# Input and memory projections in plain fp32, block transposes over 128 partitions, and one more complex product on GpSimd, in an S5 and gated-delta encoder layer

## The chip, the cores and the metric

The kernel runs on one core of a Trainium2 chip. The metric is the device time of one execution in microseconds (us). Names of engines: PE is TensorE's matmul stream and PEld its weight loads, DVE is VectorE, ACT is ScalarE, POOL is GpSimd, SP is SyncE, whose queue (SPq) issues most transfers.

## What is computed

One encoder layer on 512 tokens of width 1024, all in fp32. The part that the change touches, cut to what matters:

```python
h = rmsnorm(x, norm_mix)
u, q, k, v, z, beta_f, beta_b, a_f, a_b = split_cols(h @ w_in)   # 512, 4 x 512, 16 gate columns
y_s5  = s5_mixer(u, ...)     # two complex scans over time (forward, backward), gelu, GLU
y_gdn = gdn_mixer(q, k, v, z, beta_f, ...)   # conv of 5 taps, silu, l2norm; per chunk of 64 tokens:
#   l_mat = strict_lower(k_beta @ k.T) * decay
#   u_c, w_c = triangular_solve(l_mat, v_beta), triangular_solve(l_mat, k_beta * exp(g))
#   then a recurrence over the chunks, in both directions
x = x + concat([y_s5, y_gdn]) @ w_out
x = x + mem_xattn(rmsnorm(x, norm_xattn), rmsnorm(mem, norm_mem), wq, wk, wv, wo)   # mem: 256 x 1024
x = x + hier_moe(rmsnorm(x, norm_moe), ...)   # 32 experts, top 2 in the top group
return rmsnorm(x, norm_final)
```

## The kernel before

The order of each engine's instructions is set by the tile framework's scheduler, which starts from the program's order; several generators are interleaved into that by `weave` (L42). So the order is decided anew whenever the program changes.

**Stage A** (`stage_a`, `rms_T` L107): the tokens are loaded, normed and transposed on PE, 8 blocks of 128 features. Each block leaves PSUM twice: ACT writes it rounded to fp32r (`hth`, L129), DVE writes the rest (`htl`, L130).

**Projections.** A projection (`proj`, L180) makes 128 columns of h @ w_in for all 512 tokens. `wsplit` (L135) loads 128 columns of weights (512 KB) through SP's queue into `wst` (two buffers), ACT casts them to fp32r (`whi`, L142), and DVE or POOL subtracts (`wlo`, L143). Which of the two is set by `lo_eng`: POOL for the first two and in the memory units, DVE for the convolutions' projections. `mm3` (L146) then does three fp32r matmuls for each of 8 blocks of features: L150 (whi with htl), L151 (whi with hth), L152 (wlo with hth), 24 in all. There are 20 projections: 4 of u, 12 of q, k and v, and 4 of z. The gates (L540) are 16 matmuls with fp32 operands over `htl` and `hth`, four at a time in row groups of PE's columns.

**S5 parameters** (`s5_params`): among much else a loop of 8 turns, each with two complex products (`cmul`, L221, six operations of 128x512, L225 to L230), `pm` and `ca`. The tables `CA_ENG` and `PM_ENG` (L54) say which engine does one: 0 is DVE, 1 is POOL. Woven with it are the convolutions of q, k and v (`gdn_conv`: PE's projection, two evictions on ACT, four DVE operations at L641, silu on ACT).

**Triangular inverse** (`gdn_inv`, L686): the matrix N is built from the keys; the 32x32 diagonal blocks are transposed on DVE (`NT`, L731, four transposes, one for each 32 partitions), inverted by a recursion of 31 steps on DVE (a product, L739, and a subtraction, L741), and the result is transposed again (`XT` L748, `XN` L749, four each). PE then makes the off-diagonal blocks (L767 on) and the chain can begin. Woven with it are the S5 recursion (`s5_rec`, four small DVE operations a step, L414 to L417), the z projections, and the memory units.

**Memory units** (`mem_kv`, L945): 16 units, each 128 columns of the memory's keys or values: one `wsplit` with the subtraction on POOL, 24 fp32r matmuls of 256 columns with `mth` and `mtl`, an eviction, for values two transposes, and a store (L962, on SP's queue). The units that aren't done by then are woven with the chain.

**Chain** (`gdn_chain`, L839 on): the recurrence over chunks, small matmuls with evictions between. After it and the last memory unit a stack of pools closes (`r1`, with the weights and the memory's tiles); S5's output (`s5_out`, L446) loads `tz` (L430) into the space. Then follow the GLU (L475, fp32 matmuls), the mixing product, the cross-attention (whose own split, `wsplit4`, is another function) and the MoE, whose weights are streamed in.

Of the kernel before, what the change touches and what calls it, by code (L numbers as in the profile page):

```python
# [9 lines left out]
F32 = mybir.dt.float32  # L10
F32R = mybir.dt.float32r
BF16 = mybir.dt.bfloat16
I32 = mybir.dt.int32
U32 = mybir.dt.uint32
AF = mybir.ActivationFunctionType
OP = mybir.AluOpType
# [15 lines left out]
P = 128  # L32
T = 512
D = 1024
# [16 lines left out]
            live.remove(s)  # L51


CA_ENG = (0, 1, 0, 1, 0, 1, 0, 1)  # L54
PM_ENG = (1, 0, 1, 0, 1, 0, 1, 0)


class Enc:
    def __init__(self, ctx, tc, A, out):
        self.ctx, self.tc, self.nc, self.A, self.out = ctx, tc, tc.nc, A, out  # L60
        self.lo_eng = self.nc.vector
        self.banks, self.turn = {}, {}
        self.loads = []

# [39 lines left out]
        return t  # L104


    def rms_T(self, pool, tiles, gain, hi, lo, tag, between=None, junk=None):  # L107

        nc = self.nc
        n = len(tiles)  # L110
        ss = pool.tile([P, 8], F32, name=tag + "ss", bufs=1)
        rs = pool.tile([P, 8], F32, name=tag + "rs", bufs=1)
        xn = []
        for i, t in enumerate(tiles):
            sq = junk if junk is not None else pool.tile([P, D], BF16, name=tag + "sq", bufs=1)
            nc.scalar.activation(sq, t, AF.Square, accum_out=ss[:, i:i + 1])
            nc.vector.tensor_scalar(ss[:, i:i + 1], ss[:, i:i + 1], 1.0 / D, 1e-6, op0=OP.mult, op1=OP.add)
            nc.gpsimd.tensor_tensor(rs[:, i:i + 1], ss[:, i:i + 1], self.nhalf[:, 0:1], op=OP.pow)
            nc.vector.tensor_scalar(t, t, rs[:, i:i + 1], None, op0=OP.mult)
            xn.append(t)  # L120
        if between:
            between()
        for k in range(8):
            ps = self.ps("tp")
            for i in range(n):
                nc.tensor.transpose(ps[:, i * P:(i + 1) * P],
                                    xn[i].rearrange("t (p k) -> t k p", k=8)[:, k, :], self.ident)
            src = ps[:, :n * P]
            nc.scalar.activation(hi[:, k, :], src, AF.Copy, scale=gain[:, k:k + 1])  # L129
            nc.vector.scalar_tensor_tensor(lo[:, k, :], src, gain[:, k:k + 1], hi[:, k, :].bitcast(F32),  # L130
                                           op0=OP.mult, op1=OP.subtract)
        return xn


    def wsplit(self, src, w, lo_eng=None, tag="w"):  # L135

        nc, wp = self.nc, self.wp
        st = wp.tile([P, 8, w], F32, name="wst", tag=tag + "st", bufs=2)
        nc.sync.dma_start(st, src)
        hi = wp.tile([P, 8, w], F32R, name="whi", tag=tag + "hi", bufs=2)  # L140
        lo = wp.tile([P, 8, w], F32R, name="wlo", tag=tag + "lo", bufs=2)
        nc.scalar.activation(hi, st, AF.Copy)  # L142
        (lo_eng or self.lo_eng).tensor_tensor(lo, st, hi.bitcast(F32), op=OP.subtract)  # L143
        return hi, lo

    def mm3(self, ps, pairs, first=True, last=True):  # L146

# [7 lines left out]
    def stage_a(self):  # L155
        nc, tc, A = self.nc, self.tc, self.A
        pool = self.pa
        gain = self.col8('norm_mix', self.cp)
        x2d = A['x'][0]
        xt = []  # L160
        with tc.tile_pool(name="xp", bufs=1) as xp:
            for i in range(4):
                t = xp.tile([P, D], F32, name=f"x{i}")
                nc.sync.dma_start(t, x2d[i * P:(i + 1) * P, :])
                xt.append(t)
            self.hth = pool.tile([P, 8, T], F32R, name="hth")
            self.htl = pool.tile([P, 8, T], F32R, name="htl")
            self.pre = {}

            def first_weights():  # L170
                for c0 in (0, P):
                    self.pre[c0] = self.wsplit(self.w_in(c0, P), P, nc.gpsimd)
                self.w_g = self.wp.tile([P, 8, 16], F32, name="wg", bufs=1)
                nc.sync.dma_start(self.w_g, self.w_in(2560, 16))

            self.rms_T(xp, xt, gain, self.hth, self.htl, "h", first_weights)

    def w_in(self, c0, w):
        return self.A['w_in'][0].rearrange("(p k) n -> p k n", k=8)[:, :, c0:c0 + w]

    def proj(self, c0):

        hi, lo = self.pre.get(c0) or self.wsplit(self.w_in(c0, P), P)
        ps = self.ps("mm")
        self.mm3(ps, [((hi[:, k, :], lo[:, k, :]), (self.hth[:, k, :], self.htl[:, k, :])) for k in range(8)])
        return ps

    def proj_u(self):
# [328 lines left out]
    def gates(self):  # L517
        nc, A, tc = self.nc, self.A, self.tc
        v = nc.vector
# [4 lines left out]
        with tc.tile_pool(name="gt_", bufs=1) as tp:  # L524
# [6 lines left out]
            ps = self.ps("s5")  # L531
# [2 lines left out]
            sel = tp.tile([P, 16], F32, name="gsel")  # L534
            v.tensor_reduce(sel, self.ident.rearrange("p (i c) -> p c i", i=4)[:, :16], axis=AX.X, op=OP.add)
            for j in range(2):
                for part in (self.htl, self.hth):
                    for i in range(4):
                        k = j * 4 + i
                        nc.tensor.matmul(ps[i * 32:i * 32 + 16], self.w_g[:, k], part[:, k].bitcast(F32),  # L540
                                         start=(j == 0 and part is self.htl), stop=(j == 1 and part is self.hth))
            for i in range(4):
                nc.scalar.activation(gT[i * 32:i * 32 + 16], ps[i * 32:i * 32 + 16], AF.Copy)
            pt = self.ps("tp")
# [4 lines left out]
            y, ab, e, w, t1 = (tp.tile([P, 4, 8], F32, name="s" + n) for n in "yaewt")  # L549
# [42 lines left out]
            for hf in range(2):  # L592
                s = slice(hf * 64, hf * 64 + 64)
                f, b = slice(hf, 8, 2), slice(7 - hf, None, -2)
# [92 lines left out]
    def gdn_inv(self):  # L687
        nc, tc = self.nc, self.tc
# [4 lines left out]
        if True:  # L693
# [31 lines left out]
            Ni = N.rearrange("p d b h f -> p (d b h) f")  # L725
            NT = tp.tile([P, 32, 32], F32, name="NT", tag="NT")
            X = tp.tile([P, 32, 32], F32, name="X", tag="X")
            for q in range(4):
                s = slice(q * 32, q * 32 + 32)
                b = q % 2  # L730
                v.transpose(NT[s], Ni[s, :, b * 32:b * 32 + 32].rearrange("p i f -> p f i"))  # L731
            ii = tp.tile([P, 32, 32], I32, name="ii", tag="pd")
            g_.iota(ii, pattern=[[1, 32], [-1, 32]], base=0, channel_multiplier=0)
            v.tensor_scalar(X, ii, 0.0, None, op0=OP.is_equal)
# [8 lines left out]
                    yield  # L743
            XT = tp.tile([P, 32, 32], F32, name="XT", tag="NT")
            XN = tp.tile([P, 32, 32], F32, name="XN", tag="pd")
            for q in range(4):
                s = slice(q * 32, q * 32 + 32)
                v.transpose(XT[s].rearrange("p n i -> p i n"), X[s])  # L748
                v.transpose(XN[s].rearrange("p n j -> p j n"), X[s].rearrange("p i j -> p j i"))  # L749

            R = tp.tile([P, 32, 32], F32, name="R", tag="X")
            lh = self.lhc.rearrange("p n h (e c) -> p n h e c", e=2)
# [180 lines left out]
    def mem_norm(self):  # L933
        nc, A = self.nc, self.A
        gain = self.col8('norm_mem', self.cp)
        self.mth = self.mp.tile([P, 8, 256], F32R, name="mth")
        self.mtl = self.mp.tile([P, 8, 256], F32R, name="mtl")

        place = self.U.rearrange("p k r g -> p (k r g)")
        mt = [place[:, i * D:(i + 1) * D] for i in range(2)]  # L940
        for i, t in enumerate(mt):
            nc.sync.dma_start(t, A['mem'][0, i * P:(i + 1) * P, :])
        self.rms_T(self.mp, mt, gain, self.mth, self.mtl, "m", junk=place[:, 2 * D:2 * D + D // 2].bitcast(BF16))

    def mem_kv(self):  # L945
        nc, A, tc = self.nc, self.A, self.tc
        wk = A['xa_wk'][0].rearrange("(p k) n -> p k n", k=8)
        wv = A['xa_wv'][0].rearrange("(p k) n -> p k n", k=8)
        for which, w in ((0, wk), (1, wv)):
            for n in range(8):  # L950
                hi, lo = self.wsplit(w[:, :, n * P:(n + 1) * P], P, nc.gpsimd)
                ps = self.ps("mm")
                self.mm3(ps[:, :256], [((hi[:, k], lo[:, k]), (self.mth[:, k], self.mtl[:, k])) for k in range(8)])
                o = self.wp.tile([P, 256], F32, name="kvo", bufs=2)
                nc.scalar.activation(o, ps[:, :256], AF.Copy)
                if which:
                    pt = self.ps("tp")
                    for m in range(2):
                        nc.tensor.transpose(pt[:, m * P:(m + 1) * P], o[:, m * P:(m + 1) * P], self.ident)
                    o = self.wp.tile([P, 256], F32, name="kvt", bufs=2)  # L960
                    nc.scalar.activation(o, pt[:, :256], AF.Copy)
                nc.sync.dma_start(self.kv_scr[which, :, n], o)  # L962
                yield
# [548 lines left out]
    def build(self):  # L1512
# [41 lines left out]
        with tc.tile_pool(name="gi", bufs=2) as gi:  # L1554
            qkv = self.gdn_in([(w, n, h) for h in range(4) for w, n in ((1, "k"), (0, "q"))] +
                              [(2, "v", h) for h in range(4)], gi)
            s5 = self.s5_params()
            self.lo_eng = nc.gpsimd
            next(s5)
            for _ in u:  # L1560
                pass
            self.lo_eng = nc.vector
            weave((qkv, 13), (s5, 9))

        self.lo_eng = nc.gpsimd
        self.gp2 = pool(left, "gp2")
        self.gp3 = pool(left, "gp3")
        self.gv = pool(gv, "gv", **rt)
# [196 lines left out]
```

## Time and profile before

| what | us |
|---|---|
| median of 3 runs | 927.62 (926.51 to 932.28) |
| the profiled execution | 929.45 |
| its span in the trace | 927.3 |
| mean granted TensorE clock | 0.903 of full speed |

A row of the page or of the trace gives times from the start of the span. Busy time is time in which an engine worked on an instruction; PE's is modelled, since matmuls are pipelined. PEclk is the granted clock as a share of full speed. In brackets behind an instruction stands how long its engine was idle before it and what ended that.

### The profile page before, as it was taken

The page shows a single profiled execution, that of the slowest core. Times are in us where ns is not written, and L with a number is a line of the kernel's source. Part 1 is how long each engine was busy: PE and PEld are TensorE (multiplying, and loading weights), DVE is VectorE, ACT ScalarE, POOL GpSimd, SP SyncE. Part 2 cuts the span into 40 slices and gives each one's busy share as a digit, 9 for nine tenths or more (in the row PEclk, how much of TensorE's full clock was granted, in tenths as well). Part 3 has the DMA queues.
Part 4 walks back from the last instruction along what each step waited for, and adds up shares of the span by engine and source line. Part 5 has one row for each costly group of instructions (what it writes and reads, how often), then busy time and mean ns, then how long its engine had stood idle before and what let it go on. Part 6 is the DMA issues. An engine that isn't in the chain of part 4 may idle for free. (4 is left out here: it accounts for less than half of the span.)

```text
span 927.3 us, 13626 instructions
## 1 busy us (share of the span) xinstructions
PE 781.3 (84%) x5023; PEld 547.1 (59%) x5024; DVE 471.9 (51%) x1060; ACT 367.2 (40%) x801; POOL 302.0 (33%) x254
## 2 busy tenths in 40 slices
PE   5898898898772998899899999996699798778791
PEld 4586576677672975677488888996333343233230
DVE  5599989879999975224653444414300110010026
ACT  6555356565432534633551654432232321121123
POOL 3234687634461411200452223232311111010026
PEclk9998798999896787959899999998799999898896
DMA  8855222222451207611763623597799999999952
GB/s 205 140 86 123 94 92 71 84 60 70 120 168 53 76 18 137 137 46 47 234 215 114 245 96 121 183 405 290 269 394 409 414 412 406 404 406 403 410 223 116
DMA packets 129029, 185.39 MB, mean 200 GB/s; under 512 B 38818, under 2 KB 93090, under 8 KB 125120
## 3 DMA queue, kind: packets, MB, share of 16 engines
q1 hardware_dynamic: 124640, 176.50, 56.7%
q0 software_dynamic: 4320, 8.00, 2.4%
q8 instruction: 40, 0.66, 0.3%
q14 instruction: 29, 0.24, 0.1%
HBM read 165.50 MB, written 26.71 MB: 207 GB/s over the span
## 5 line engine op out<-in xcount | busy, mean ns | idle before, releaser
L1344 PE MATMUL bank<-mw,xt 128*64 128x512 f32 x400 | 114.1, 609 | 1.7 <-ACT yd L1390 1.3
L1348 DVE SCALAR_TENSOR_TENSOR hs<-hs,tw,bank 128x256 f32<-128x256 f32 x16 | 7.7, 480 | 173.1 <-ACT hs L1347 173.1
L143 POOL TENSOR_TENSOR wlo<-wst,whi 128x1024 fp32r<-128x1024 f32 x24 | 58.0, 2420 | 57.6 <-ACT whi L142 44.7
L150 PE MATMUL bank<-htl,whi 128*128 128x512 f32 x160 | 69.3, 434 | 6.2 <-ACT cv L639 3.1
L1344 PEld LDWEIGHTS bank<-mw,xt 128*64 128x64 f32 x400 | 38.5, 143 | 55.9 <-issue 49.9
L152 PE MATMUL bank<-hth,wlo 128*128 128x512 f32 x160 | 67.4, 422 | 0.3 <-DVE wlo L143 0.3
L151 PE MATMUL bank<-hth,whi 128*128 128x512 f32 x160 | 67.2, 420 | 0.0
L973 POOL TENSOR_TENSOR wlo<-wst,whi 128x1024 fp32r<-128x1024 f32 x16 | 38.4, 2404 | 80.8 <-ACT whi L972 80.8
L1347 ACT ACTIVATE hs<-bank,tw 128x256 f32<-128x256 f32 x16 | 7.6, 473 | 137.1 <-PE bank L1344 137.1
L1385 PE MATMUL bank<-mw,hT 128*64 128x512 f32 x120 | 45.7, 664 | 10.9 <-DMA mw<-in_moe_w_down_dram 9.3
L1324 POOL DMA_INDIRECT xg<-t_scr,tidx x16 | 16.4, 1024 | 115.7 <-PE bank L1331 101.4
L142 ACT ACTIVATE whi<-wst 128x1024 fp32r<-128x1024 f32 x36 | 38.2, 1060 | 28.2 <-DMA wst<-in_w_in_dram 9.9
L641 DVE SCALAR_TENSOR_TENSOR cv<-xp,taps,cv 128x512 f32<-128x512 f32 x48 | 46.5, 971 | 0.4
L152 PE MATMUL bank<-mth,wlo 128*128 128x256 f32 x128 | 40.1, 313 | 7.7 <-POOL wlo L143 7.7
L1391 POOL DMA_INDIRECT y_scr<-yd,didx x14 | 14.0, 1001 | 93.5 <-ACT yd L1390 25.0
L150 PE MATMUL bank<-mtl,whi 128*128 128x256 f32 x128 | 40.0, 312 | 3.4 <-ACT zt L683 3.4
L150 PEld LDWEIGHTS bank<-htl,whi 128*128 128x128 f32 x160 | 33.1, 207 | 14.4 <-ACT cv L639 3.8
L1334 ACT ACTIVATE xt<-bank,gm 128x128 f32<-128x128 f32 x128 | 35.0, 391 | 15.4 <-PE bank L1331 15.1
L151 PE MATMUL bank<-mth,whi 128*128 128x256 f32 x128 | 38.9, 304 | 0.0
L152 PEld LDWEIGHTS bank<-hth,wlo 128*128 128x128 f32 x160 | 32.6, 204 | 8.2 <-DVE wlo L143 0.7
L151 PEld LDWEIGHTS bank<-hth,whi 128*128 128x128 f32 x160 | 33.0, 206 | 6.7 <-issue 0.2
L150 PE MATMUL bank<-wlo,oh 128*128 128x256 f32 x128 | 36.6, 289 | 0.0
(570 smaller groups left out, 2219.9 us busy)
## 6 DMA issues: line engine op xcount, KB each, us to landing
mw<-in_moe_w_gate_dram SPq DMA_DIRECT2D x50, 512.0 KB, 13.0
mw<-in_moe_w_up_dram SPq DMA_DIRECT2D x50, 512.0 KB, 12.6
mw<-in_moe_w_down_dram SPq DMA_DIRECT2D x15, 1024.0 KB, 13.8
wst<-in_w_in_dram SPq DMA_DIRECT2D x20, 512.0 KB, 4.3
xl<-in_moe_w_down_dram SPq DMA_DIRECT2D x5, 1024.0 KB, 12.1
ol<-in_moe_w_down_dram SPq DMA_DIRECT2D x5, 1024.0 KB, 13.7
xh<-in_moe_w_down_dram SPq DMA_DIRECT2D x5, 1024.0 KB, 13.3
ca_scr<-ca SPq DMA_DIRECT2D x8, 512.0 KB, 2.7
```

The source lines that it names most:

```text
L142: nc.scalar.activation(hi, st, AF.Copy)
L143: (lo_eng or self.lo_eng).tensor_tensor(lo, st, hi.bitcast(F32), op=OP.subtract)
L150: self.nc.tensor.matmul(ps, ah, bl, start=(first and i == 0), stop=False)
L151: self.nc.tensor.matmul(ps, ah, bh, start=False, stop=False)
L152: self.nc.tensor.matmul(ps, al, bh, start=False, stop=(last and i == n - 1))
L641: v.scalar_tensor_tensor(cv, xp[:, w:w + T], taps[:, w, m:m + 1], cv, op0=OP.mult, op1=OP.add)
L973: nc.gpsimd.tensor_tensor(lo, st, hi.bitcast(F32), op=OP.subtract)
L1324: self.gather = g_.indirect_dma_start(out=xg, out_offset=None, in_=self.t_scr, in_offset=bass.IndirectOffsetOnAxis(ap=self.tidx[:, q:q + 1 ...
L1334: nc.scalar.activation(xt[:, k], ps[:, (k % 4) * P:(k % 4 + 1) * P], AF.Copy, scale=self.gm[:, k:k + 1])
L1344: nc.tensor.matmul(pg[w * 64:w * 64 + 64].rearrange("p (a n) -> p a n", a=2), xt[:, k, w * 64:w * 64 + 64], un[k // 4 * 2 + w][:, :, k % 4 ...
L1385: nc.tensor.matmul(py[w * 64:w * 64 + 64], hT[:, k, w * 64:w * 64 + 64], wd[w][:, k, c], start=(k == 0), stop=(k == 1))
L1391: nc.gpsimd.indirect_dma_start(out=self.y_scr, out_offset=bass.IndirectOffsetOnAxis(ap=self.didx[:, q:q + 1], axis=0), in_=y, in_offset=No ...
```

## The change

`rms_T` writes one fp32 tile (`ht`, `mt`) in place of a pair; its evictions alternate between ACT and DVE. `wcols` only loads the weights, into four buffers in place of two. `mm8` does 8 fp32 matmuls in place of the 24 of `mm3`; the gates take 8 matmuls in place of 16. The casts and subtractions of weights in projections and memory units go, and with them `lo_eng`. `NT` takes three transposes (one of 128 partitions, two of 32), `XT` and `XN` one of 128 partitions each. In the S5 loop POOL does nine of the 16 complex products in place of eight. The split products of the cross-attention and the mixing stay.

```diff
-CA_ENG = (0, 1, 0, 1, 0, 1, 0, 1)
-PM_ENG = (1, 0, 1, 0, 1, 0, 1, 0)
+CA_ENG = (1, 1, 0, 1, 1, 1, 0, 1)
+PM_ENG = (0, 0, 1, 0, 1, 0, 1, 0)
...
-            nc.scalar.activation(hi[:, k, :], src, AF.Copy, scale=gain[:, k:k + 1])
-            nc.vector.scalar_tensor_tensor(lo[:, k, :], src, gain[:, k:k + 1], hi[:, k, :].bitcast(F32),
-                                           op0=OP.mult, op1=OP.subtract)
+            if k % 2:
+                nc.vector.tensor_scalar(out[:, k, :], src, gain[:, k:k + 1], None, op0=OP.mult)
+            else:
+                nc.scalar.activation(out[:, k, :], src, AF.Copy, scale=gain[:, k:k + 1])
...
-    def wsplit(self, src, w, lo_eng=None, tag="w"):
-
-        nc, wp = self.nc, self.wp
-        st = wp.tile([P, 8, w], F32, name="wst", tag=tag + "st", bufs=2)
-        nc.sync.dma_start(st, src)
-        hi = wp.tile([P, 8, w], F32R, name="whi", tag=tag + "hi", bufs=2)
-        lo = wp.tile([P, 8, w], F32R, name="wlo", tag=tag + "lo", bufs=2)
-        nc.scalar.activation(hi, st, AF.Copy)
-        (lo_eng or self.lo_eng).tensor_tensor(lo, st, hi.bitcast(F32), op=OP.subtract)
-        return hi, lo
+    def wcols(self, src, w):
+
+        t = self.wp.tile([P, 8, w], F32, name="wst", bufs=4)
+        self.nc.sync.dma_start(t, src)
+        return t
+
+    def mm8(self, ps, w, act):
+
+        for k in range(8):
+            self.nc.tensor.matmul(ps, w[:, k, :], act[:, k, :], start=(k == 0), stop=(k == 7))
...
-        self.mm3(ps, [((hi[:, k, :], lo[:, k, :]), (self.hth[:, k, :], self.htl[:, k, :])) for k in range(8)])
+        self.mm8(ps, w, self.ht)
...
-                for part in (self.htl, self.hth):
-                    for i in range(4):
-                        k = j * 4 + i
-                        nc.tensor.matmul(ps[i * 32:i * 32 + 16], self.w_g[:, k], part[:, k].bitcast(F32),
-                                         start=(j == 0 and part is self.htl), stop=(j == 1 and part is self.hth))
+                for i in range(4):
+                    k = j * 4 + i
+                    nc.tensor.matmul(ps[i * 32:i * 32 + 16], self.w_g[:, k], self.ht[:, k], start=(j == 0), stop=(j == 1))
...
-            for q in range(4):
+            nd = lambda b: Ni[:, :, b * 32:b * 32 + 32].rearrange("p i f -> p f i")
+            v.transpose(NT, nd(0))
+            for q in (1, 3):
                 s = slice(q * 32, q * 32 + 32)
-                b = q % 2
-                v.transpose(NT[s], Ni[s, :, b * 32:b * 32 + 32].rearrange("p i f -> p f i"))
+                v.transpose(NT[s], nd(1)[s])
...
-            for q in range(4):
-                s = slice(q * 32, q * 32 + 32)
-                v.transpose(XT[s].rearrange("p n i -> p i n"), X[s])
-                v.transpose(XN[s].rearrange("p n j -> p j n"), X[s].rearrange("p i j -> p j i"))
+            v.transpose(XT.rearrange("p n i -> p i n"), X)
+            v.transpose(XN.rearrange("p n j -> p j n"), X.rearrange("p i j -> p j i"))
...
-                hi, lo = self.wsplit(w[:, :, n * P:(n + 1) * P], P, nc.gpsimd)
                 ps = self.ps("mm")
-                self.mm3(ps[:, :256], [((hi[:, k], lo[:, k]), (self.mth[:, k], self.mtl[:, k])) for k in range(8)])
+                self.mm8(ps[:, :256], self.wcols(w[:, :, n * P:(n + 1) * P], P), self.mt)
```

## Rows read from the trace of the kernel before

**Rows 1.** The page's first part: busy us of each engine, its share of the span, and its number of instructions.

```profile
PE 781.3 (84%) x5023; PEld 547.1 (59%) x5024; DVE 471.9 (51%) x1060; ACT 367.2 (40%) x801; POOL 302.0 (33%) x254
```

**Rows 2.** The table of windows: from and to, length, then busy us and number of instructions of PE, PEld, DVE, ACT and POOL, then PEclk, the DMA engines' mean busy share, and GB/s.

```profile
16.00:40.70 24.70, 21.40 (x116) 15.03 (x114) 12.49 (x36) 11.04 (x18) 6.53 (x5) 1.00 0.87 137
40.70:72.00 31.30, 30.94 (x137) 25.29 (x137) 30.05 (x98) 17.55 (x32) 11.56 (x12) 0.95 0.65 100
...
16.00:238.00 222.00, 194.24 (x1508) 150.02 (x1506) 190.57 (x379) 122.44 (x257) 115.00 (x97) 0.92 0.40 92
246.00:293.00 47.00, 28.98 (x224) 27.14 (x222) 47.00 (x147) 13.04 (x19) 21.81 (x9) 0.90 0.42 122
293.00:317.00 24.00, 18.08 (x308) 17.36 (x308) 23.30 (x32) 12.60 (x22) 6.22 (x4) 0.71 0.29 86
317.00:464.00 147.00, 133.27 (x879) 99.80 (x880) 75.17 (x213) 63.75 (x134) 33.40 (x48) 0.81 0.40 101
600.00:927.00 327.00, 261.01 (x1332) 128.50 (x1330) 60.10 (x144) 81.49 (x237) 68.43 (x59) 0.91 0.90 354
```

**Rows 3.** DVE's timeline in 246 to 293 us: start, duration, engine, line, operation, output and inputs, shapes. The first and the last row are the recursion's first product and last subtraction.

```profile
246.17 0.18 DVE L739 TENSOR_TENSOR pd<-NT,X 128x31 f32<-128x31 f32 x1
...
251.14 2.42 DVE L414 TENSOR_TENSOR rt<-a8r,U 128x64 f32<-128x64 f32 x1
...
254.56 0.21 DVE L414 TENSOR_TENSOR rt<-a8r,U 128x64 f32<-128x64 f32 x1
...
292.45 0.18 DVE L741 TENSOR_TENSOR X<-X,pd 128x31 f32<-128x31 f32 x1
```

**Rows 4.** POOL's timeline in the same stretch.

```profile
251.04 2.45 POOL L143 TENSOR_TENSOR wlo<-wst,whi 128x1024 fp32r<-128x1024 f32 x1 [0.44 <-ACT whi L142]
```

**Rows 5.** The weights' subtraction (L143). The first row is POOL's group in the table by line for 246 to 293 us, the second DVE's group in that for 40.7 to 196: shapes, number, busy us and mean ns, idle time before. The third is POOL's row in the tile's own view: number, shortest, median and longest ns, first and last start.

```profile
L143 POOL TENSOR_TENSOR wlo<-wst,whi 128x1024 fp32r<-128x1024 f32 x9 | 21.8, 2423 | 16.8 <-ACT whi L142 16.8
...
L143 DVE TENSOR_TENSOR wlo<-wst,whi 128x1024 fp32r<-128x1024 f32 x12 | 17.6, 1468 | 4.2 <-ACT whi L142 4.2
...
L143 POOL TENSOR_TENSOR wlo<-wst,whi x24: 2334/2378/2853, 11.9 to 324.8; 128x1024 fp32r<-128x1024 f32 x24
```

**Rows 6.** Transposes and other block operations on DVE and POOL. The first row is from DVE's timeline (four transposes one after the other in 7.89 us), the others from the views of single tiles and lines, with number, shortest, median and longest ns, first and last start, and from the timeline again.

```profile
237.98 7.89 DVE L731 STREAM_TRANSPOSE NT<-N 32x1024 f32<-32x1024 f32 x4
...
L748 DVE STREAM_TRANSPOSE XT<-X x4: 1885/1915/2059, 292.7 to 304.1; 32x1024 f32<-32x1024 f32 x4
L749 DVE STREAM_TRANSPOSE XN<-X x4: 1921/2020/2046, 294.5 to 306.0; 32x1024 f32<-32x1024 f32 x4
...
L656 DVE TENSOR_TENSOR vc<-bank,beta x8: 672/688/695, 192.7 to 225.1; 64x512 f32<-64x512 f32 x8
...
170.12 0.68 DVE L227 TENSOR_TENSOR pm<-aF,b 128x512 f32<-128x512 f32 x1
...
L230 POOL TENSOR_TENSOR ca<-ca,P x4: 1712/1724/1737, 91.8 to 179.3; 128x512 f32<-128x512 f32 x4
L230 DVE TENSOR_TENSOR ca<-ca,P x4: 679/1134/1768, 77.2 to 164.4; 128x512 f32<-128x512 f32 x4
```

**Rows 7.** PE's timeline after the recursion: start, duration of the group, and in brackets the idle time before it and what ended that.

```profile
298.37 3.62 PE L767 MATMUL bank<-XT,N 32*32 32x32 f32 x64 [17.25 <-DVE XT L748]
...
306.32 2.21 PE L767 MATMUL bank<-XT,N 32*32 32x32 f32 x64
...
317.43 0.77 PE L839 MATMUL bank<-vc,lhc 128*128 128x128 f32 x2 [0.97 <-ACT whi L142]
```

**Rows 8.** PE's timeline in three places: 23 matmuls of a split projection that follow on each other (the first and the last of them), 17 of a memory unit (the first and the last), and fp32 matmuls of the GLU, 8 records; then the GLU's row in the line's own view (number of records, shortest, median and longest ns).

```profile
196.58 0.39 PE L151 MATMUL bank<-hth,whi 128*128 128x512 f32 x1
...
201.59 0.39 PE L152 MATMUL bank<-hth,wlo 128*128 128x512 f32 x1
...
247.11 0.28 PE L152 MATMUL bank<-mth,wlo 128*128 128x256 f32 x1
...
249.02 0.28 PE L150 MATMUL bank<-mtl,whi 128*128 128x256 f32 x1
...
448.96 3.70 PE L475 MATMUL bank<-gt,wglu 128*128 128x512 f32 x8
...
L475 PE MATMUL bank<-gt,wglu x32: 592/592/1062, 438.3 to 463.0; 128*128 128x512 f32 x32
```

**Rows 9.** PE's timeline: the first and the last of the gates' four groups.

```profile
27.77 1.05 PE L540 MATMUL bank<-htl,wg 128*16 128x512 f32 x8
...
30.36 1.04 PE L540 MATMUL bank<-hth,wg 128*16 128x512 f32 x8
```

**Rows 10.** The view of the tile `htl` on PE in 16 to 72 us: the projections' matmuls with their number, shortest, median and longest ns, first and last start.

```profile
L150 PE MATMUL bank<-htl,whi x56: 387/389/776, 16.1 to 71.1; 128*128 128x512 f32 x56
```

**Rows 11.** The table of windows for PE's matmuls on `mtl` alone, 8 of them to a memory unit: window, length, their busy us and number, PEclk, DMA share, GB/s.

```profile
238.00:293.00 55.00, 23.82 (x80) 0.86 0.41 122
293.00:317.00 24.00, 5.39 (x16) 0.71 0.29 86
317.00:345.00 28.00, 8.50 (x24) 0.80 0.07 23
```

**Rows 12.** The queue of SP and PE's timeline where S5's output begins.

```profile
347.95 3.93 SPq L430 DMA_DIRECT2D tz<-w_scr  x8
...
360.14 1.09 PE L446 MATMUL bank<-tz,uperm 128*64 128x128 f32 x4 [4.41 <-DMA tz<-w_scr]
```

More of the change, by code (lines that the diff above doesn't have):

```diff
@@ L60, in __init__ @@
         self.ctx, self.tc, self.nc, self.A, self.out = ctx, tc, tc.nc, A, out
-        self.lo_eng = self.nc.vector
         self.banks, self.turn = {}, {}
@@ L104, in colt, with rms_T @@
         return t
-    def rms_T(self, pool, tiles, gain, hi, lo, tag, between=None, junk=None):
+    def rms_T(self, pool, tiles, gain, out, tag, between=None, junk=None):
         nc = self.nc
@@ L165, in stage_a @@
                 xt.append(t)
-            self.hth = pool.tile([P, 8, T], F32R, name="hth")
-            self.htl = pool.tile([P, 8, T], F32R, name="htl")
+            self.ht = pool.tile([P, 8, T], F32, name="ht")
             self.pre = {}
@@ L171, in first_weights @@
                 for c0 in (0, P):
-                    self.pre[c0] = self.wsplit(self.w_in(c0, P), P, nc.gpsimd)
+                    self.pre[c0] = self.wcols(self.w_in(c0, P), P)
                 self.w_g = self.wp.tile([P, 8, 16], F32, name="wg", bufs=1)
                 nc.sync.dma_start(self.w_g, self.w_in(2560, 16))
-            self.rms_T(xp, xt, gain, self.hth, self.htl, "h", first_weights)
+            self.rms_T(xp, xt, gain, self.ht, "h", first_weights)
     def w_in(self, c0, w):
@@ L181, in proj @@
     def proj(self, c0):
-        hi, lo = self.pre.get(c0) or self.wsplit(self.w_in(c0, P), P)
+        w = self.pre.pop(c0, None)
+        if w is None:
+            w = self.wcols(self.w_in(c0, P), P)
         ps = self.ps("mm")
-        self.mm3(ps, [((hi[:, k, :], lo[:, k, :]), (self.hth[:, k, :], self.htl[:, k, :])) for k in range(8)])
+        self.mm8(ps, w, self.ht)
         return ps
@@ L935, in mem_norm @@
         gain = self.col8('norm_mem', self.cp)
-        self.mth = self.mp.tile([P, 8, 256], F32R, name="mth")
-        self.mtl = self.mp.tile([P, 8, 256], F32R, name="mtl")
+        self.mt = self.mp.tile([P, 8, 256], F32, name="mt")
         place = self.U.rearrange("p k r g -> p (k r g)")
@@ L942, in mem_norm @@
             nc.sync.dma_start(t, A['mem'][0, i * P:(i + 1) * P, :])
-        self.rms_T(self.mp, mt, gain, self.mth, self.mtl, "m", junk=place[:, 2 * D:2 * D + D // 2].bitcast(BF16))
+        self.rms_T(self.mp, mt, gain, self.mt, "m", junk=place[:, 2 * D:2 * D + D // 2].bitcast(BF16))
     def mem_kv(self):
@@ L1557, in build @@
             s5 = self.s5_params()
-            self.lo_eng = nc.gpsimd
             next(s5)
@@ L1561, in build @@
                 pass
-            self.lo_eng = nc.vector
             weave((qkv, 13), (s5, 9))
-        self.lo_eng = nc.gpsimd
         self.gp2 = pool(left, "gp2")
```

## The prediction

> **What bounds the kernel now.** I read the busy shares of the page first: TensorE (PE) leads, but four engines share the work [rows 1]. An average over unlike stages says little, so next came the table of windows, one row a stage [rows 2]. In 16–238 us (projections, S5 parameters, convolutions) PE and VectorE (DVE) are both nearly full: PE 194.24 of 222 at a mean granted clock of 0.92, DVE 190.57. In 246–293 DVE alone sets the time: 47.00 of 47.00 busy, PE 28.98. In 293–317 DVE still leads (23.30 of 24). In 317–464, the chunk chain, PE is the fullest with 133.27 of 147 at clock 0.81. From 600 to 927 the DMA share is 0.90: the expert weights bound it, and this stage, whose code the change leaves alone, keeps its length and only starts earlier or later.
>
> Second I looked at DVE's timeline in 246–293, to see whether those 47 us are its own work. They aren't. The recursion runs from 246.17 to 292.63 [rows 3], and where a POOL subtraction of weights (`wlo`, L143) starts at 251.04 for 2.45 us, the DVE product of L414 started at 251.14 lasts 2.42 us; the same product alone lasts 0.21 [rows 3, 4]. Nine such subtractions of 2423 ns lie in the window [rows 5].
>
> Third, what follows the recursion: PE's L767 waits 17.25 us for the transposes, and the chain's first matmul stands behind it at 317.43 [rows 7].
>
> **The change, part by part.**
>
> *TensorE, projections.* A split projection is 24 matmuls of 512 columns. 22 intervals between 196.58 and 201.59 give 0.228 us each, so 5.46 us [rows 8]. Its replacement is 8 plain fp32 matmuls. The nearest row is the fp32 matmul of L475, of the same shape: 8 records in 3.70 us, the last lasting 0.59, so (3.70−0.59)/7 = 0.444 us a record. The 16 matmuls of L475 leave 32 records, so two make one matmul: 0.89 us, 8 make 7.1 us. That is +1.6 us a projection, +32 for 20. The gates (L540) issue 16 matmuls in four groups, from 27.77 to 30.36, so 0.86 us a group [rows 9]; two groups go, −1.7.
>
> *TensorE, memory units.* 16 intervals of 256 columns from 247.11 to 249.02 give 0.119 us [rows 8], 2.87 us for 24. No row has fp32 at 256 columns. From below 2 × 0.119 a matmul, 1.9 us a unit; from above the 512-column price, 7.1. I take a little over half of the latter, since columns halve: 3.7 us, +0.8 a unit.
> The Trainium skill (FP8 and Floating Point Precision, TensorE Precision Notes) says that true FP32 takes four passes through the array; by it a unit would be 8 × 4 × 0.119 = 3.8 us, an estimate. At 512 columns it would be 8 × 4 × 0.228 = 7.3, and the row's 7.1 agrees within 3%.
>
> *Stage 16–238.* Seven projections (56 matmuls of their `htl` product, 8 to each) lie in 16–72 [rows 10], where PE is busy 52.34 of 56.0 us [rows 2]: there the extra is paid, 11 us. In the rest DVE is fullest, and it loses 12 subtractions, 17.6 us [rows 5], and one complex product of six operations (0.7 to 1.8 us each beside POOL; rows 6 have both engines' durations), about 7 us. So PE decides the stage. Its work at full clock is about 194.24 × 0.92 = 179; with 32 − 1.7 it is 209. Before, 27.8 us of idle time and 15.5 of clock stood on top. I let a third of both stay, since PE has fewer producers to wait for (no `whi`, no `wlo`, four load buffers) and DVE's late convolutions come sooner: 209 + 14 = 223, so +1. Ends: none stays, −13; all stays, 30.3/0.92 = +33.
> What I cost at nothing here: POOL's extra product (about 6 × 1.7 = 10 us, covered as POOL is busy 115.00 of 222; if it ends a turn of the S5 loop last, up to +10, which lies inside the upper end); the evictions of `rms_T`, eight an engine becoming four (at best they bring the first matmul 3 us forward, at worst nothing); the 36 casts on ACT, busy 122.44 of 222 [rows 2]; and the loads, same bytes on the same SP queue, issued earlier with four buffers.
>
> *NT.* Four transposes of 32 partitions took 7.89 us; three remain (one of 128 partitions, two of 32). No row has a transpose over 128 partitions. From below, a price as for 32 (1.97 us); from above, four times that. The nearest fact: other DVE operations cost the same on 64 and 128 partitions, 688 and 680 ns for 512 elements [rows 6]. I take 1.97: −2.0. The upper end is +3.9.
> The Trainium skill (Vector Engine (DVE) Microarchitecture Reference, 3.8) puts a 32 by 32 transposing array in front of each 32-channel bank; by it four banks would work side by side, again 2 us. No row here shows that.
>
> *Recursion.* Its nine POOL subtractions vanish. Each holds one DVE operation up for about 2.42 − 0.21 = 2.2 us: −19.7 of 46.5 [rows 3 to 5]. Ends: 0 if DVE is held up by something else in those places, −21.8.
>
> *XT and XN.* Eight transposes of 32 partitions, 292.7 to 308.0 us, become two: 15.3 − 3.9 = −11.4 for DVE [rows 6]. PE used the second part of that time for L767's first half; the chain's start follows the last transposes, so I take −10. At four times the price: 0.
>
> *Chain.* POOL's subtractions go on to 324.8 [rows 5], so the chain's first steps meet one or two of them: −1 (0 to −3).
>
> *Memory units pushed back.* Ten of the 16 units ran in 238–293 (80 matmuls on `mtl`, 8 a unit), two in 293–317, three in 317–345 [rows 11], one earlier. The first stage shrinks to about 33 us, which holds 8 or 9 at 3.7. With one earlier and two in the next stage, about five then fall into the chain's stage, not three: 5 × 3.7 − 3 × 2.87 = +10. PE is the fullest there, so most of it counts: +8. Late next is the first `tz` load (L430, on SP's queue), which waits for pools that close after the last unit: it goes out at 347.95, and PE's L446 waits 4.41 us for it at 360.14 with chain matmuls queued behind [rows 12]. Ends: 0, if all fit earlier, and +21, if seven come at clock 0.80.
>
> *Sum.* +1 − 2.0 − 19.7 − 10 − 1 + 8 = −23.7. The profiled execution took 929.45 us (its span 927.3 and 2.15 around it): 905.8. It lies 1.8 above the median of 927.62, so on the median 904.
>
> **The rivals.**
>
> *PE becomes the bound and nothing gives way* (the other side). The gaps in 16–238 are dependencies of the convolutions and the S5 turns, not DVE load, and the clock stays 0.92: +33. The units in the chain at clock 0.80 are 5 × 3.7/0.80 − 3 × 2.87/0.80 = +12. Against the gains of −32.7 that is +12: 942 profiled, 940 on the median. For it: PE's 52.34 of 56.0 in 16–72. Against: in 72–238 DVE is the fuller engine and is relieved. It decides once more than 33 of some 45 added PE us reach the end. Chance 0.13.
>
> *The units eat the recursion's gain.* Seven units spill, +21 instead of +8: 917. For: PE is full in the chain. Against: without `wlo`, units no longer wait for POOL. Chance 0.16.
>
> *Transposes cost by partition.* NT +3.9 instead of −2, XT/XN 0 instead of −10: +16, so 920. Chance 0.12.
>
> *The stage 16–238 gets shorter.* No gap and no clock loss stays: −13 instead of +1, so 890. For: DVE sheds 25 us. Chance 0.16.
>
> *The forecast*, 904: chance 0.43, its own range 890 to 917.
>
> **How the numbers follow.** One per cent, about what a measurement of this kernel can tell from no change, puts the bounds at 918.3 and 936.9. Below lie nearly all of the forecast and the short stage, over half of the spilled units and about 0.4 of the transposes: 0.42 + 0.16 + 0.10 + 0.05, less 0.02 for the unlisted: 0.71. Above lies most of the first rival, 0.11. Between, 0.18. The range: 880, some way under the shortest case, to 930, which leaves out the first rival and little else.
>
> **What would show it.** The recursion (L739, L741) lasts about 27 us with no row of 2.4 us on DVE. A transpose of 128x1024 takes about 2.0 us (7.8: the third rival). Fp32 records come 0.44 us apart at 512 columns and about 0.23 at 256. NT starts near 239 (270 by the first rival, 225 by the fourth), with PE's clock over 0.95. The chain starts near 287, and 40 matmuls' worth of units follow it (56 by the second rival). From the chain's start to the end the length stays, but for the units. I'd be wrong if the order of work, which is decided anew, moved the z projections or the units to places that these rows don't show.

## The result, and the profile after

The changed kernel takes 901.77 us (median of 4 runs, 898.18 to 905.82), the kernel before 927.07 beside it: a ratio of 0.974, 95% interval 0.968 to 0.980. Its profiled execution took 905.82 us, span 904.1, against 929.45 and 927.3: 23.6 less. The first part of the page, which answers to [rows 1], shows PE as the only engine with more to do; DVE lost 77 us and POOL 59.

```profile
PE 790.3 (87%) x4719; PEld 497.9 (55%) x4720; DVE 395.3 (44%) x1027; ACT 327.4 (36%) x757; POOL 242.8 (27%) x236
```

The table of windows, stage by stage, with the columns of [rows 2]: 16 us to the start of NT, the recursion, the inverse's products, and from the chain's start to the end of the GLU.

```profile
16.00:244.00 228.00, 211.50 (x1314) 111.96 (x1314) 163.69 (x399) 100.68 (x231) 95.14 (x95) 0.95 0.39 91
...
250.30:277.00 26.70, 22.93 (x107) 19.84 (x105) 26.70 (x144) 2.30 (x6) 0.00 (x0) 1.00 0.65 192
277.00:300.00 23.00, 20.86 (x292) 18.94 (x293) 16.43 (x53) 9.75 (x18) 3.12 (x4) 0.70 0.16 49
...
300.00:445.00 145.00, 133.67 (x946) 100.43 (x945) 58.60 (x147) 66.18 (x141) 29.77 (x45) 0.94 0.47 121
```

The same window of the kernel before, from its chain's start to the end of its GLU (the row of [rows 2] ends 9 us sooner):

```profile
317.00:473.00 156.00, 142.27 (x928) 107.37 (x929) 79.08 (x220) 68.27 (x141) 35.63 (x49) 0.82 0.42 108
```

DVE's timeline after, at the first product and the last subtraction of the recursion (as [rows 3]):

```profile
250.32 0.18 DVE L738 TENSOR_TENSOR pd<-NT,X 128x31 f32<-128x31 f32 x1
...
276.88 0.18 DVE L740 TENSOR_TENSOR X<-X,pd 128x31 f32<-128x31 f32 x1
```

It lasts 26.7 us in place of 46.5, with POOL idle. The transposes, each tile's own view (as [rows 6]):

```profile
L730 DVE STREAM_TRANSPOSE NT<-N x2: 1934/1936/1937, 246.1 to 248.1; 32x1024 f32<-32x1024 f32 x2
L727 DVE STREAM_TRANSPOSE NT<-N x1: 1971/1971/1971, 244.0 to 244.0; 128x1024 f32<-128x1024 f32 x1
...
L745 DVE STREAM_TRANSPOSE XT<-X x1: 1898/1898/1898, 277.1 to 277.1; 128x1024 f32<-128x1024 f32 x1
...
L746 DVE STREAM_TRANSPOSE XN<-X x1: 1971/1971/1971, 278.9 to 278.9; 128x1024 f32<-128x1024 f32 x1
```

PE's timeline from the end of stage one to the chain's start (as [rows 7, 8]):

```profile
235.02 7.13 PE L143 MATMUL bank<-ht,wst 128*128 128x512 f32 x16
241.99 31.24 PE L143 MATMUL bank<-mt,wst 128*128 128x256 f32 x144
...
279.14 6.82 PE L764 MATMUL bank<-XT,N 32*32 32x32 f32 x128 [5.91 <-issue]
285.89 0.69 PE L954 MATMUL bank<-ident,kvo 128*128 128x128 f32 x2
286.37 6.26 PE L143 MATMUL bank<-mt,wst 128*128 128x256 f32 x16
292.57 1.10 PE L772 MATMUL bank<-R,XN 32*32 32x32 f32 x29
...
300.17 0.39 PE L836 MATMUL bank<-vc,lhc 128*128 128x128 f32 x2
```

A projection takes 7.13 us. Nine memory units run back to back, 31.24/9 = 3.47 us each. Then PE idles 5.9 us, the clock falls (0.70 in 277–300), and a unit of 6.26 us stands between the inverse's two products. The last square sums of the GLU, in the line's view, before and then after, mark its end:

```profile
L483 PE MATMUL bank<-ones,s5q x32: 164/250/373, 446.2 to 472.7; 128*128 128x1 f32 x32
```

```profile
L483 PE MATMUL bank<-ones,s5q x32: 164/250/271, 413.0 to 445.0; 128*128 128x1 f32 x32
```

Where the 23.6 us are, from these rows and those of before:

| stretch | before | after | change | forecast |
|---|---|---|---|---|
| 16 us to NT | 222.0 | 228.0 | +6.0 | +1 |
| NT | 8.2 | 6.3 | −1.9 | −2.0 |
| recursion | 46.5 | 26.7 | −19.7 | −19.7 |
| its end to the chain's start | 24.8 | 23.1 | −1.7 | −10 |
| chain's start to the GLU's end | 155.3 | 144.8 | −10.4 | +7 |
| the rest, to the span's end | 454.6 | 459.1 | +4.5 | 0 |
| around the span | 2.15 | 1.72 | −0.4 | 0 |

So the total was right and three terms weren't. The rest lasted 452 to 468 us in the profiled executions of kernels that have the same code there; its +4.5 lies within that.

### The profile page after: what moved, and what is told of

Its sections match the earlier page's. It is cut to its first block, busy times and chain, and to the rows that moved or that the text cites. A ratio compares the mean times of both kernels' runs of the same rounds, so it can differ in the third digit from the quotient of the medians.

```text
span 904.1 us, 12927 instructions
## 1 busy us (share of the span) xinstructions
PE 790.3 (87%) x4719; PEld 497.9 (55%) x4720; DVE 395.3 (44%) x1027; ACT 327.4 (36%) x757; POOL 242.8 (27%) x236
## 5 line engine op out<-in xcount | busy, mean ns | idle before, releaser
L143 PE MATMUL bank<-ht,wst 128*128 128x512 f32 x320 | 153.0, 626 | 2.4 <-ACT kd L583 2.4
L143 PEld LDWEIGHTS bank<-ht,wst 128*128 128x128 f32 x320 | 61.0, 199 | 71.8 <-issue 68.3
L143 PE MATMUL bank<-mt,wst 128*128 128x256 f32 x256 | 59.8, 392 | 0.0
L968 POOL TENSOR_TENSOR wlo<-wst,whi 128x1024 fp32r<-128x1024 f32 x16 | 38.4, 2403 | 79.3 <-ACT whi L967 79.3
L143 PEld LDWEIGHTS bank<-mt,wst 128*128 128x128 f32 x256 | 49.9, 198 | 7.7 <-issue 0.8
L820 POOL TENSOR_TENSOR kt<-kn,kd 64x512 f32<-64x512 f32 x14 | 14.5, 1035 | 97.6 <-PE bank L774 51.4
L150 PE MATMUL bank<-whi,oh 128*128 128x256 f32 x128 | 35.8, 283 | 0.0
L850 DVE SCALAR_TENSOR_TENSOR S<-S,egl,bank 128x128 f32<-128x128 f32 x48 | 15.5, 345 | 45.8 <-PE bank L847 45.8
L151 PE MATMUL bank<-whi,ol 128*128 128x256 f32 x128 | 35.3, 287 | 0.0
L1380 PE MATMUL bank<-xl,hT 128*64 128x512 f32 x40 | 20.5, 646 | 7.0 <-DMA xl<-in_moe_w_down_dram 4.2
```

What stands on the lines that cost most here:

```text
L143: self.nc.tensor.matmul(ps, w[:, k, :], act[:, k, :], start=(k == 0), stop=(k == 7))
L150: self.nc.tensor.matmul(ps, ah, bh, start=False, stop=False)
L151: self.nc.tensor.matmul(ps, al, bh, start=False, stop=(last and i == n - 1))
L820: nc.gpsimd.tensor_tensor(kt[s], self.kn[s, ch // 2], self.kd[s, ch // 2, di * 4:di * 4 + 4, None].to_broadcast([64, 4, P]), op=OP.mult)
L850: v.scalar_tensor_tensor(sn, S[di, h], self.egl[:, ch % 2, ch // 2, di * 4 + h:di * 4 + h + 1], p, op0=OP.mult, op1=OP.add)
L968: nc.gpsimd.tensor_tensor(lo, st, hi.bitcast(F32), op=OP.subtract)
```

## The experiments

Each was timed beside the kernel before, whose median lay between 922.5 and 928.3 us, so ratios are the thing to compare; the changed kernel's is 0.974 (0.968 to 0.980). "NT at" is the start of its first transpose; before 238.0, changed kernel 244.0. It is read from one trace of each kernel: the changed kernel and four others with its code ahead of NT have it at 243.5 to 246.4.

**The memory units alone.** On the kernel before; projections still split. Only the core of the edit is shown; it also gives the projections' loads four buffers and the memory's features one fp32 tile.

```diff
-                hi, lo = self.wsplit(w[:, :, n * P:(n + 1) * P], P, nc.gpsimd)
...
+                self.mm8(ps[:, :256], self.wcols(w[:, :, n * P:(n + 1) * P], P), self.mt)
```

> The kernel before with the memory units alone changed: plain fp32, four load buffers, no cast and no subtraction; projections, gates, transposes and tables as before. Theory (POOL's two-input subtraction holds DVE up): the recursion L739/L741 falls from 46.5 us to about 27 with the transposes untouched, the start of NT stays near 238, and the kernel is 14 to 20 us shorter than before (907 to 913). Rival (something else holds those DVE operations up): the recursion stays over 40 us and the time within 5 us of 927.

Measured: 897.02 us, ratio 0.970 (0.965 to 0.974). NT at 238.9, recursion 26.7 us with all transposes old. This one part brings as much as the whole change, more than was expected: the chain's start came 27.5 us after the recursion's end (24.8 before), but the stretch behind it, to the GLU's end, was shorter, as in the changed kernel: 134.9 us at a granted clock of 0.94, with four units in it.

**An idle POOL subtraction beside each unit.** On the changed kernel:

```diff
+                wd = self.wp.tile([P, 8, P], F32, name="wd", bufs=2)
+                nc.gpsimd.tensor_tensor(wd, wt, wt, op=OP.subtract)
```

> The changed kernel with one idle POOL subtraction of 128x1024 added to each memory unit, read by nobody. Theory (POOL's two-input operation holds DVE up for its whole length): each of the seven or eight that fall into the recursion adds about 2.2 us, the recursion grows from 26.8 to about 43 us, the kernel by 10 to 16 (912 to 918). Rival (the cast, the wait or the loads made the recursion long): recursion within 3 us of 26.8, time within 3 of 902.

Measured: 916.53 us, ratio 0.990 (0.986 to 0.994); the recursion 40.4 us, with eight POOL operations in it. POOL's and DVE's timelines of this run (DVE's first and last row are the recursion's first product and last subtraction):

```profile
261.24 1.90 POOL L950 TENSOR_TENSOR wd<-wst 128x1024 f32<-128x1024 f32 x1 [1.54 <-DMA wst<-in_xa_wk_dram]
```

```profile
253.89 0.18 DVE L738 TENSOR_TENSOR pd<-NT,X 128x31 f32<-128x31 f32 x1
...
261.31 1.91 DVE L414 TENSOR_TENSOR rt<-a8r,U 128x64 f32<-128x64 f32 x1
...
294.07 0.18 DVE L740 TENSOR_TENSOR X<-X,pd 128x31 f32<-128x31 f32 x1
```

A DVE operation of 0.22 us lasts as long as the POOL operation beside it, and nobody reads what POOL makes. Eight of them at 1.9 − 0.2 us are 13.6, and the recursion is 13.7 longer. The recursion's gain is this hold-up; the rival falls.

**The old transposes.** On the changed kernel, the twelve of before (NT's four aren't shown).

```diff
...
-            v.transpose(XT.rearrange("p n i -> p i n"), X)
-            v.transpose(XN.rearrange("p n j -> p j n"), X.rearrange("p i j -> p j i"))
+            for q in range(4):
+                s = slice(q * 32, q * 32 + 32)
+                v.transpose(XT[s].rearrange("p n i -> p i n"), X[s])
+                v.transpose(XN[s].rearrange("p n j -> p j n"), X[s].rearrange("p i j -> p j i"))
```

> The changed kernel with the twelve transposes of 32 partitions back (NT four, XT and XN eight). As the prediction has it: +12 (2 for NT, 10 for XT and XN), about 914. Theory from the trace after (the inverse stage is held by PE, at half clock and with a memory unit in front of its second product, so that most of what DVE saves is lost): +2 to +5, 904 to 907.

Measured: 904.99 us, ratio 0.977 (0.972 to 0.981), which can't be told from the changed kernel. In the traces NT takes 7.9 us and the chain starts 27.2 us after the recursion's end, 23.1 in the changed kernel. So XT and XN bring 4.1 us of the 10 forecast. A second pair of runs agrees: with split projections and the old tables (further down) the new transposes take this stretch from 27.5 to 22.5. Both kernels with fp32 units and old transposes are at 27 us, above the 24.8 of before: the units had made the stretch longer first.

**More units ahead of the inverse.**

```diff
-            yield from itertools.islice(kv, 8)
+            yield from itertools.islice(kv, 11)
...
-        weave((inv, 16), (rest(), 13), (itertools.islice(rec, 16), 17))
+        weave((inv, 16), (rest(), 16), (itertools.islice(rec, 16), 17))
```

> The changed kernel with eleven memory units in place of eight woven in ahead of the inverse's products (two numbers in the program's order). Theory (after the recursion PE idles 5.9 us, falls to half clock, and then has a memory unit in front of the second product): the idle time is filled, no unit stands between L764 and L772, the chain starts some 8 us sooner after the recursion's end (15 in place of 23), fewer units follow it, and the kernel is 4 to 8 us shorter than the changed one. Rival (PE's work only moves): within 2 us of it.

Measured: 904.63 us, ratio 0.980 (0.976 to 0.984). PE's timeline:

```profile
278.59 6.66 PE L764 MATMUL bank<-XT,N 32*32 32x32 f32 x125 [4.63 <-issue]
285.20 1.73 PE L772 MATMUL bank<-R,XN 32*32 32x32 f32 x29
...
289.32 2.07 PE L143 MATMUL bank<-mt,wst 128*128 128x256 f32 x4
291.32 1.91 PE L772 MATMUL bank<-R,XN 32*32 32x32 f32 x32
293.16 5.60 PE L143 MATMUL bank<-mt,wst 128*128 128x256 f32 x14
```

No unit stands ahead of L772 any more, but units moved in behind it, the idle time stayed (4.63 us), and the chain began at 304.2, 27.7 us after the recursion's end. My theory's repair failed: the chain's stage held four units in place of five, but the work only moved, as the rival has it, and the ratio is no better than the changed kernel's.

**Shorter units in the chain.** The last four units do two of eight products: it leaves out three quarters of the features of half the memory's values, so the routing of tokens behind it differs as well.

```diff
...
+                self.mm8(ps[:, :256], self.wcols(w[:, :, n * P:(n + 1) * P], P), self.mt, 2 if which and n > 3 else 8)
```

> The changed kernel with two in place of eight products in each of the last four memory units (values 512 to 1023 of the memory are sums over a quarter of the features): it leaves out 24 fp32 products of 256 columns, 24 x 0.43 = 10.4 us of PE's work behind the chain's start. Theory (PE bounds the chain, the memory units pushed into it are paid there): 7 to 10 us shorter than the changed kernel. Rival (the chain waits on its own evictions and hides the units): within 2 us of it.

Measured: 896.50 us, ratio 0.968 (0.962 to 0.974): 5 us less, between the two, and the intervals overlap. The chain's start to the GLU's end shows it without the routing: 300.7 to 430.6, 129.9 us against 144.8.

```profile
300.70:430.60 129.90, 122.06 (x868) 90.31 (x868) 52.73 (x142) 66.27 (x140) 29.59 (x45) 0.90 0.50 125
```

PE is 11 us less busy there for 10.4 us of products left out. The other kernels with five units behind the chain's start take 139.5 to 147.5 us, so all of them are longer, by 10 to 18: these units are paid in about full. That they cost more than their own time isn't shown.

**Split projections again.** On the changed kernel, the 20 projections and the gates as before, with the casts and subtractions that belong to them (only the products are shown).

```diff
...
-        self.mm8(ps, w, self.ht)
+        self.mm3(ps, [((hi[:, k, :], lo[:, k, :]), (self.hth[:, k, :], self.htl[:, k, :])) for k in range(8)])
```

> The changed kernel, but with the 20 projections and the gates split as before (casts on ACT, subtractions on DVE, 24 fp32r matmuls); memory units, transposes and tables as changed. Theory (PE bounds 16 us to NT, and plain fp32 costs it more there than the relief of DVE gives back): NT starts near 238 in place of 244, and the kernel is 4 to 8 us shorter than the changed one (894 to 898). Rival (the relief of DVE pays for it): NT starts at 244 or later, the time 902 to 910.

Measured: 902.91 us, ratio 0.975 (0.970 to 0.980), NT at 248.4: the rival's side, and a puzzle, as the memory units alone had NT at 238.9 with the same projections. Only the tables lie ahead of NT between the two, so two runs went to them.

**The old tables**, once on the changed kernel and once on the one with split projections.

```diff
-CA_ENG = (1, 1, 0, 1, 1, 1, 0, 1)
-PM_ENG = (0, 0, 1, 0, 1, 0, 1, 0)
+CA_ENG = (0, 1, 0, 1, 0, 1, 0, 1)
+PM_ENG = (1, 0, 1, 0, 1, 0, 1, 0)
```

> The changed kernel with the tables of the S5 loop as before: eight complex products on POOL, taking turns with DVE. As the prediction has it: the ninth product on POOL is hidden, so within 2 us of the changed kernel. Theory from the run that split the projections again (its NT started at 248.4, that of the memory units alone at 238.9, and of what differs between the two only the tables lie ahead of NT): the new tables cost up to 9 us there; NT starts 3 to 9 us sooner than at 244.0 and the kernel is that much shorter.

> The kernel before with the memory units and the twelve transposes changed, all else as before: split projections and gates, old tables. It differs from the run with the new tables and split projections only in the tables, and from the run of the memory units alone only in the transposes. Theory (the tables cost that run its 9 us): NT starts near 239, and with three transposes in NT the time is 2 to 3 us below the 897.0 of the memory units alone, 893 to 896. Rival (the order of the work fell out badly in that run, for no one part): NT at 244 or later, 900 or more.

Measured: on the changed kernel 895.02 us, ratio 0.969 (0.965 to 0.972), NT at 238.6; with split projections 892.68, 0.967 (0.963 to 0.971), NT at 237.8. So the tables put NT off by 5.4 and 10.6 us: the ninth product isn't hidden. (In each pair the two ratios' intervals overlap; it is the traces that show it.) The changed kernel's PE shows where a part of it arises, against the one with the old tables:

```profile
142.32 0.63 PE L381 MATMUL bank<-ca,bb 64*32 64x128 f32 x2 [4.03 <-POOL xp L634]
142.88 7.26 PE L143 MATMUL bank<-ht,wst 128*128 128x512 f32 x10
```

```profile
138.33 0.66 PE L381 MATMUL bank<-ca,bb 64*32 64x128 f32 x16
138.93 7.13 PE L143 MATMUL bank<-ht,wst 128*128 128x512 f32 x16
```

The same 20 us in the table of windows, changed kernel and old tables:

```profile
137.00:157.00 20.00, 15.73 (x101) 8.07 (x100) 15.09 (x19) 9.93 (x32) 13.14 (x14) 0.83 0.19 62
```

```profile
137.00:157.00 20.00, 18.66 (x119) 10.05 (x118) 14.47 (x25) 10.60 (x34) 5.53 (x9) 1.00 0.28 84
```

In that turn, the fifth, both products are POOL's, and PE waits 4 us for the second (the row names a memset that POOL does right behind it). Behind the wait the granted clock is lower: ten records take 7.26 us, where the old tables' kernel does 16 in 7.13. With the old tables no wait on POOL stands there, and DVE's last copy of `wl` (L387), which ends the loop, starts at 195.7 in place of 199.8.

With the old tables NT is at 238.6 with fp32 projections and at 237.8 with split ones. The stage's rows:

```profile
16.00:238.60 222.60, 205.80 (x1321) 110.43 (x1320) 163.65 (x400) 99.64 (x229) 87.53 (x90) 0.97 0.41 94
```

```profile
16.00:237.80 221.80, 189.42 (x1501) 147.40 (x1500) 182.25 (x376) 119.75 (x253) 107.72 (x97) 0.93 0.41 96
```

So 16 us more of PE's busy time, 23 at full clock (205.80 × 0.97 against 189.42 × 0.93, an estimate), move NT by 0.8: idle time and clock loss fall by as much.

**Two load buffers.**

```diff
-        t = self.wp.tile([P, 8, w], F32, name="wst", bufs=4)
+        t = self.wp.tile([P, 8, w], F32, name="wst", bufs=2)
```

> The changed kernel with two load buffers for the weights in place of four. Theory (a load of 512 KB takes 4.3 us to land and a memory unit now lasts 3.5 us on PE, so two buffers can't keep PE fed in the recursion): PE waits on loads there, fewer units fit in before the chain, 2 to 8 us longer than the changed kernel. Rival (the loads were hidden with two): within 2 us.

Measured: 886.86 us, ratio 0.961 (0.956 to 0.965), NT at 233.0. Both theories missed: fewer buffers are faster by 1.3%, clear of both intervals. The reason stands in the changed kernel's trace. SP's queue, then ACT's timeline:

```profile
26.86 1.29 SPq L137 DMA_DIRECT2D wst<-in_w_in_dram  x2
28.19 1.11 SPq L102 DMA_DIRECT2D c_norm_xattn<-in_norm_xattn_dram  x1
29.47 6.11 SPq L609 DMA_DIRECT2D taps<-in_gdn_conv_dram  x5
35.68 1.72 SPq L137 DMA_DIRECT2D wst<-in_w_in_dram  x1
37.51 0.59 SPq L195 DMA_DIRECT2D u_scr<-ut  x1
```

```profile
32.98 1.05 ACT L194 ACTIVATE ut<-bank 128x512 f32<-128x512 f32 x1
...
42.16 1.06 ACT L194 ACTIVATE ut<-bank 128x512 f32<-128x512 f32 x1 [5.94 <-DMA u_scr<-ut]
...
43.66 0.22 ACT L213 ACTIVATE ft<-fr 128x32 f32<-128x32 f32 x1
```

The first u is evicted by 34.0, but its store is issued at 37.51, behind three weight loads; with two buffers one stands there, and the store goes out at 32.88. The second eviction waits for it, and the S5 parameters' tanh (L213) is queued behind that on ACT. In the kernel before, and with split projections and four load buffers, the tanh stands ahead of the second eviction (it starts at 41.45, and at 40.4 to 41.5): so the loss isn't that of the buffers alone.

**A second buffer for u, four load buffers kept.**

```diff
-            u = self.wp.tile([P, 8, 64], F32, name="ut", tag="ut", bufs=1)
+            u = self.wp.tile([P, 8, 64], F32, name="ut", tag="ut", bufs=2)
...
-            z = self.wp.tile([P, T], F32, name="zt", tag="ut", bufs=1)
+            z = self.wp.tile([P, T], F32, name="zt", tag="ut", bufs=2)
```

> The changed kernel with two buffers in place of one for the tile that ACT evicts u into (and z, which shares its tag); four load buffers stay. Theory (in the changed kernel the second eviction of u on ACT waits 5.94 us for the store of the first, whose issue on SP's queue stands behind five small loads and three more weight loads that the four buffers let ahead; S5's tanh is queued behind it on ACT): the wait goes, the S5 parameters come 4 to 5 us sooner, NT starts at 238 to 241 in place of 244.0, the time is 3 to 6 us below the changed kernel. Rival (the wait is hidden, the later turns of the S5 loop set NT): NT within 2 us of 244.

Measured: 889.16 us, ratio 0.961 (0.956 to 0.966), NT at 232.3. ACT's timeline:

```profile
32.26 2.17 ACT L194 ACTIVATE ut<-bank 128x512 f32<-128x512 f32 x2
...
36.12 0.22 ACT L213 ACTIVATE ft<-fr 128x32 f32<-128x32 f32 x1
```

The wait was the cause, and it cost twice what I expected: the tanh comes 7.5 us sooner, NT 11.7. The edit gives z a second buffer too, but in the changed kernel's trace no eviction of z waits for a store. How the delay grows on its way through the S5 turns, whose order was decided anew as well, is argued from the two traces only.

**Together.** Old tables and two load buffers, and with u's second buffer too.

> The changed kernel with the old tables and two load buffers, the two single changes that made it faster each. If they act in different places and add up: NT starts near 228, the time is about 20 us below the changed kernel, near 880. Rival (both work on the same chain of S5 turns ahead of NT): NT at 233 or later as with two buffers alone, 885 to 890.

> The changed kernel with the old tables, two load buffers and two buffers for u's tile together. If the store of u still holds ACT with two load buffers (2.38 us there): 1 to 3 us below the run with the first two alone; if not, the same within 1 us.

Measured: 887.49 us, ratio 0.957 (0.952 to 0.963), NT at 229.5; and 883.43, 0.954 (0.948 to 0.959), NT at 228.7. At NT the first two nearly add up (−14.5 against −5.4 and −11.0 alone), but 887.49 can't be told from two buffers alone, and u's second buffer brings 4 us more, with overlapping intervals. The kernel with all three beats both of the study's: 2% under the changed one, 4.6% under the one before.

## Why the prediction was right, point by point

- **Recursion**: −19.7 forecast, −19.7 measured; that POOL causes it is shown by the idle subtraction, which puts 13.7 us back with eight operations of 1.9 us (before, nine of 2.4).
- **Prices**: a projection 7.13 us (7.1), a unit 3.47 (3.7), a transpose over 128 partitions 1.90 to 1.97 (1.97), NT −1.9 (−2.0). The rival of transposes by partition falls. The Trainium skill (FP8 and Floating Point Precision, TensorE Precision Notes) has true FP32 in four passes; the estimate from that was 3.8 for a unit, and the measured 3.47 decides. The Trainium skill (Vector Engine (DVE) Microarchitecture Reference, 3.8) has a transposing array in front of each 32-channel bank; the 1.90 to 1.97 us for four banks, as long as for one, agree with that.
- **XT and XN**: the step "the chain's start follows the last transposes, so I take −10" failed. With the transposes over by 280.9, PE follows later: idle time, a lower clock, a unit in front. They are worth 4.1 to 5.0 us to the chain's start; the other part of the stretch is that fp32 units had made it longer (27.5 us with old transposes against 24.8).
- **Chain**: the units came as forecast (five behind the chain's start), and their work too. Busy time by granted clock is 142.27 × 0.82 = 117 before and 133.67 × 0.94 = 126 after, so +9; the term said +8. What I had left out is the clock: the loss at the lower level fell from 142.27 − 117 = 26 to 8 us. By this estimate it outweighs the units, and with 2 us less idle time makes the stretch 10 us shorter. The clock goes with the memory units' new form, since with that alone it is 0.94 already; why it stood higher I did not test.
- **Stage 16 to NT**: +6.0 where +1 was forecast, and for other reasons. That plain fp32 on PE is nearly free there is right (0.8 us between the two projections with the old tables). By the prediction's own sum the stage after is 211.50 × 0.95 = 201 us of work at full clock (209 forecast) and 27 of idle time and clock loss (14 forecast). The step that failed is "what I cost at nothing": the ninth product on POOL, which I bounded at +10 but took as hidden (+5.4 on the changed kernel), and "the loads, same bytes on the same SP queue, issued earlier": what they pass on that queue, u's store, was the thing to count (−11.7 when its wait is gone). The kernel before had no such wait ahead of its tanh, so −11.7 is what its removal gains, not what the change added. Without both, NT starts at 228.7, 9 us sooner than before and near the rival of the shorter stage (225). There the sum comes out: 204.99 × 0.98 = 201 and 12 us of idle time and clock loss, near the 14 that were to stay.

```profile
16.00:228.70 212.70, 204.99 (x1322) 109.97 (x1321) 162.03 (x392) 100.14 (x230) 89.39 (x90) 0.98 0.41 94
```

- **The sum**: −1.7 in place of −10 and +6.0 in place of +1 cost 13 us, the chain gave 17 back, and the rest took 4.5. The total of 904 against 901.77 owes that to errors that cancel.

Left open: what sets the clock in the chain, and how much of the tables' and the buffers' cost is the product or the wait and how much the order decided anew.

## What to carry to other kernels

Before you price an elementwise operation on POOL, look at what DVE does beside it: here that was the largest part of the gain. When a change gives loads more buffers, list what they now overtake on their queue, and which engine waits for a store behind them. And take a change of several parts apart: one part brought the whole gain, and two others each hid some 5 to 11 us of loss.

## What the runs showed of the hardware, unexpected

A DVE transpose of 128x1024 takes 1.90 to 1.97 us, one of 32x1024 1.93. A DVE operation of 0.22 us lasts 1.9 us beside a POOL subtraction of that length. An fp32 product of 256 columns takes two records of 0.217 us (31.24/144). Behind 4 us in which PE stood idle, ten fp32 records of 512 columns took 7.26 us, against 7.13 for 16 in a stretch at the full granted clock. The same memory unit took 3.47 us at the full granted clock and 6.26 in a stretch whose mean clock was 0.70. Fewer load buffers made a kernel 1.3% faster.
